# Weight blocks in rows of 2 KB, later stores and another order of reads in a gated pooling and recurrence block

## The chip, the cores and the metric

The kernel runs on one core of a Trainium2 chip. It is one launch. The metric is the device time of that launch in microseconds, the median of several runs.

## What is computed

One layer of a decoder trunk on 2048 tokens of width 1024. The token row is normalised, scaled and shifted by a condition; one wide projection (7168 columns) gives eight parts; a pooling branch and a gated linear recurrence (8 heads of 128) are each projected to the model width, merged by two sigmoid gates and projected once more. Cut to what matters:

```python
h = rms_norm(x, g_pre) * (1.0 + scale) + shift
(pv, pg, hq, hf, hi, hg, mg_pool, mg_hgrn) = jnp.split(h @ w_in, split_idx, axis=-1)

pooled = multiscale_pool(pv)                      # windows 2, 4, 8, 16: mean - token
pooled = jnp.einsum('bsgc,gcd->bsgd', pooled, pool_w).reshape(b, s, POOL_WIDTH) * pool_scale
branch_a = (pooled * jax.nn.silu(pg)) @ w_pool_o

f = lb + (1.0 - lb) * jax.nn.sigmoid(hf)
o = hgrn2(jax.nn.silu(hq), 1.0 - f, hi, jnp.log(jnp.maximum(f, 1e-30)))
o = rms_norm(o, hgrn_norm_g)                      # per head
branch_b = (o * jax.nn.silu(hg)) @ w_hgrn_o

merged = jax.nn.sigmoid(mg_pool) * branch_a + jax.nn.sigmoid(mg_hgrn) * branch_b
y = merged @ w_out
x = x + gate * rms_norm(y, g_post)
```

All inputs and the output are float32.

## The kernel before

**Products.** Each float32 operand is split in two float32r halves (`split`, L174: ScalarE casts the high half, VectorE subtracts it to get the low half), and a product is three matmuls (`three`, L337). Pairs of blocks are multiplied with seven products in place of eight (`quad`, L592, with the weight sums of `quad_items`, L211; and `rows7`, L906, for whole rows). The seven forms are called B11, B21, T1, T2, T3, B22, T4 in `rows7`.

**Stages.** The tokens are worked in two passes of 1024 (`p` 0 and 1), each with two halves `t` of 512. A pass has the value product `V`, then eight heads. A head has three quads: `fq` (forget and query), `m` (the merge gates, stored after a sigmoid by `m_got`, L864) and `gp` (gate and pooling). The recurrence of a head runs as a generator (`hgrn`, L643) that a tick moves on one step; a head has 21 ticks (`htick`, L1370). Behind the heads come the pool projection (`a_job`, L1017), the recurrence's projection (`b_job`, L1027, or `b_fast`, L1075, in the second pass) and the output product `y` (`y_fast`, L1117), in whose steps the first pass also reads and prepares the x of the second.

**Weights.** Weights come as a list of items that are used in order. `take` (L323) hands out the next one and has the items of the four after it loaded and split. In the first pass a weight block is loaded from the input (`raw_load`), split, used, and for the head quads and the pool projection also stored split (512 KB, `keep`) for the second pass, which reads it back (`again`). An item from `whole_item` (L1207) is loaded two items ahead and split when its turn comes.

**Factor steps.** The weight sums of the row products `y7` and `v7` (first pass) and `b7` (second pass) are made by `row_factors` (L256) as a list of small steps: a load of four blocks, sums and differences on VectorE, and stores to DRAM. The list `behind_heads` is worked off inside the heads, on ticks whose count modulo 5 is 1 or 3; what is left runs behind the last head.

**Order.** A planner orders the instructions of each engine; every plain DMA is issued by SP, in one queue. A store (`store`, L108) waits on SP for its data. `gated` (L111) queues a load behind the last store: `after` gives it an edge to that instruction, which holds for instructions of the same engine.

Of the kernel before, what the change touches and what calls it, by code (L numbers as in the profile page):

```python
# [8 lines left out]
F32 = mybir.dt.float32  # L9
# [9 lines left out]
P = 128  # L19
SEQ = 2048  # L20
D = 1024
T = 512
# [48 lines left out]
@with_exitstack  # L71
def tile_block(ctx: ExitStack, tc: tile.TileContext, x, c, w_ada, b_ada, g_pre, g_post, w_in,
               pool_w, pool_scale, lb_logits, hgrn_norm_g, w_pool_o, w_hgrn_o, w_out,
               ident_d, mask_d, icnt_d, w_pv_t, x_t, out):
    nc = tc.nc
    V, A, G, PE, SP = nc.vector, nc.scalar, nc.gpsimd, nc.tensor, nc.sync
    x, out = x[0], out[0]
# [87 lines left out]

    ko = "(k p) n -> p k n"
    items = []
    made = {}  # L170
    scr = {}
# [39 lines left out]
    def quad_items(key, oa, ob, keep_it):  # L211

        def make():
            base = len(ready)
            if (key, 0) in scr:
                return [lambda i=i: again((key, i), f"{base + i}") for i in range(7)]
            r = {}

            def ld(nm, o, half):
                s = w_in[:, o:o + P].rearrange("(i two p) n -> two p i n", p=P, two=2)[half]  # L220
                r[nm] = raw_load(f"{base}{nm}", (s, P))

            def one(i, nm):
                w = item_split(f"{base + i}", r[nm])
                keep((key, i), w, keep_it)
                return w

            def f0():
                if key in made:
                    r["11"], r["12"] = made.pop(key)  # L230
                else:
                    ld("11", oa, 0)
                ld("21", ob, 0)
                ld("22", ob, 1)
                if "12" not in r:
                    ld("12", oa, 1)
                return one(0, "11")

            def f1():
                r["s1"] = wrp.tile([P, T], F32, tag="wr", name=f"wr{base}s1")  # L240
                V.tensor_tensor(r["s1"], r["21"], r["22"], op=ADD)
                return one(1, "s1")

            def f2():
                V.tensor_tensor(r["21"], r["11"], r["21"], op=SUB)
                V.tensor_tensor(r["11"], r["s1"], r["11"], op=SUB)
                return one(2, "11")

            def f3():
                w = one(3, "12")  # L250
                V.tensor_tensor(r["12"], r["12"], r["11"], op=SUB)
                return w
            return [f0, f1, f2, f3, lambda: one(4, "21"), lambda: one(5, "12"), lambda: one(6, "22")]
        items.append((7, make, None))

    def row_factors(key, src, e, whole=(), skip=()):  # L256

        steps = []
        for i in range(4):
            r = {}  # L260

            def ld(i=i, r=r):
                for nm, k, z in (("11", 0, 0), ("21", 0, 1), ("12", 1, 0), ("22", 1, 1)):
                    r[nm] = utile(f"ra{key}{i}{nm}")
                    SP.dma_start(r[nm], src[(2 * i + k) * P:(2 * i + k + 1) * P, z * T:(z + 1) * T])

            def put(f, nm, i=i, r=r):
                if f in whole:
                    scr[key, f, i] = dram(f"scr_{key}_{f}_{i}", [P, T])
                    store((key, f, i), scr[key, f, i], r[nm])  # L270
                    return
                w = [utile(f"rf{key}{f}{i}{z}", F32R) for z in range(2)]
                split(r[nm], w[0], w[1], e)
                scr[key, f, i] = dram(f"scr_{key}_{f}_{i}", [P, 2 * T])
                for z in range(2):
                    store((key, f, i), scr[key, f, i][:, z * T:(z + 1) * T], w[z].bitcast(F32))

            def sums(r=r, i=i):
                r["s1"] = utile(f"rs{key}{i}")
                tt(r["s1"], r["21"], r["22"], op=ADD, e=e)  # L280

            def sub(o, a, b, r=r):
                tt(r[o], r[a], r[b], op=SUB, e=e)

            nop = lambda: None
            todo = [(None, ld), (None, nop),
                    (0, lambda put=put: put(0, "11")),
                    (None, sums),
                    (1, lambda put=put: put(1, "12")),
                    (2, lambda put=put: put(2, "s1")),  # L290
                    (None, lambda sub=sub: sub("21", "11", "21")),
                    (None, lambda sub=sub: sub("11", "s1", "11")),
                    (3, lambda put=put: put(3, "11")),
                    (4, lambda put=put: put(4, "21")),
                    (None, lambda sub=sub: sub("12", "12", "11")),
                    (5, lambda put=put: put(5, "12")),
                    (6, lambda put=put: put(6, "22"))]
            steps += [g for f, g in todo if f not in skip]
        return steps
# [564 lines left out]
    def m_got(p, j, row, t, u, cx):  # L864
        s = utile(f"sgm{p}_{j}_{row}") if t == 0 else u
        A.activation(s, u, AF.Sigmoid)
        store(("Sd", j, row), cx["Sd"][j, row][:, t, :], s)


    def v_job(p, t, grp, q, cx, hook=None):  # L870
# [246 lines left out]
    def y_fast(p, cx, more_steps):  # L1117
# [10 lines left out]
        behind = []  # L1128

        def got(n, t, tk, src):  # L1130
            if (n, t) == (0, 1):
                x_in(0, tk)
            jy = sp.tile([P, T], BF16, tag="jx", name=f"jy{p}_{t}_{n}_{tk}", bufs=1)
            A.activation(jy, src, AF.Square, scale=1.0 / 32, accum_out=rs[t][tk][:, n:n + 1])
            y = src if n == t else utile(f"y{p}_{t}_{n}_{tk}")
            iy = tt(y, src, cx["gg"][n])
            ys[t, tk, n] = y
            if n != 1 - t:
                return
            r = rs[t][tk][:, 0:1]  # L1140
            G.tensor_scalar(r, r, rs[t][tk][:, 1:2], EPS, op0=ADD, op1=ADD)
            tt(r, r, mh[:, 0:1], op=ALU.pow, e=G)

            def scale():
                tok = p * 8 + t * NT + tk
                for n2 in range(2):
                    y, xx = ys.pop((t, tk, n2)), xr[t, tk, n2]
                    V.scalar_tensor_tensor(xx, y, r, xx, op0=MUL, op1=ADD)
                    o = (out[tok * P:(tok + 1) * P, n2 * T:(n2 + 1) * T], xx)
                    if t == 1 or not fin:  # L1150
                        outs.append((state["use"], *o))
                    else:
                        while outs:
                            store("out", *outs.pop(0)[1:])
                        SP.dma_start(*o)
            with after(iy):
                while behind:
                    behind.pop()()
            behind.append(scale)

        def step(nm, i):
            next_parts(p, nm, i, "m", cx["m32"], cx)
            if nm == ("T2" if fin else "T3"):
                for tk in ((0,), (1,), (2, 3))[i]:
                    x_in(1, tk)
            if fin and (nm, i) == ("T1", 0):
                hold_last()
            more_steps(nm, i)
# [60 lines left out]
    for p in range(NPASS):  # L1229
# [11 lines left out]
                else:  # L1241
                    quad_items(("gp", h), (O_PV if h % 2 == 0 else O_PG) + (h // 2) * P, O_G + h * P, p == 0)
        for j in range(KT):
            plain_item(("a", j), w_pool_o[:, j * P:(j + 1) * P].rearrange(ko, p=P), P, p == 0)
        for j in range(KT if p < NPASS - 1 else 0):
            for half in range(2):
                plain_item(("b", j, half),
                           w_hgrn_o[half * T:(half + 1) * T, j * P:(j + 1) * P].rearrange(ko, p=P), P, False)
        if p == NPASS - 1:
            factor_items("b7")  # L1250
        factor_items("y7", p == NPASS - 1)
# [57 lines left out]
    for p in range(NPASS):  # L1309
# [60 lines left out]
        def htick():  # L1370
            tick()
            every[0] += 1
            if every[0] % 5 in (1, 3):
                once(behind_heads)

        for h in range(NH):
            if 0 < h < NH - 1:
# [40 lines left out]
                once(steps)  # L1418
            if p + 1 < NPASS:
                x_stats(8 + h)  # L1420
        while behind_heads:
            once(behind_heads)

        for j in range(KT):
            if j > 0:
# [27 lines left out]
        if p + 1 < NPASS:  # L1453
            nx = cxs[p + 1]
            early = [lambda t=t: r_row(1, t, nx) for t in range(2)]
            tks = [(t, k) for t in range(2) for k in range(KT)]

            def one(i):
                if i < 16:
                    xt_load(1, *tks[i], nx, gated)  # L1460
                if 1 < i < 18:
                    h_scale(*tks[i - 2], nx)
                if 2 < i < 3 + KT:
                    k = i - 3
                    part(1, ("B11", "B21")[k % 2], k // 2, nx["h32"][0, k], nx)

            early += [lambda i=i: one(i) for i in range(18)]

            def y_step(nm, i):
                once(early)  # L1470

            y_fast(p, cx, y_step)
            while early:
                once(early)
        else:
            y_fast(p, cx, lambda nm, i: None)
# [25 lines left out]
```

## Time and profile before

| | before |
|---|---|
| median of 3 runs | 1775.32 us |
| lowest and highest | 1771.82 and 1777.3 us |
| the profiled execution | 1774.9 us |
| its span | 1773.1 us |
| TensorE, VectorE, ScalarE busy | 98%, 69%, 47% of the span |
| mean DMA rate | 245 GB/s |

The span runs from the first to the last instruction of the profiled execution. A busy share is an average over stages, so it tells little of one stage; the table by stretches and the waits tell where an engine stood still. PE is TensorE's matmuls, PEld its weight loads, DVE is VectorE, ACT ScalarE, POOL GpSimd, and SP the engine that issues DMAs (its queue is SPq). Names such as `whl<-wr` are output and input tiles: `wr` and `wri` are raw weights, `whl` split ones, `sm` sigmoids read back from `Sd`, `xr` rows of x for the residual, `h` columns of x, `rav`, `rab` and `rsv`, `rfb` blocks and results of factor steps, `scr_` the DRAM they go to.

### The profile page before, as it was taken

The numbers are of one execution on the slowest core, as the hardware profiler recorded it, in microseconds if no ns is written. First come the engines' busy times: TensorE is split into PE (matmuls) and PEld (weight loads), VectorE is DVE, ScalarE is ACT, GpSimd is POOL, SyncE is SP. The second block draws the span as 40 slices with busy tenths as digits, with TensorE's granted clock in tenths as the row PEclk, the third lists the DMA queues.
The fourth block names the chain that finished last, engine by engine and source line by source line (L and its number), as shares of the span: only waits on it lengthen the run. The fifth ranks groups of instructions, "written<-read, shape, count | busy, mean of one in ns | idle before, by whom it ended". The sixth has DMA issues, their size and how long they took to land.

```text
span 1773.1 us, 31829 instructions
## 1 busy us (share of the span) xinstructions
PE 1729.8 (98%) x11853; PEld 1417.2 (80%) x11853; DVE 1223.7 (69%) x2538; ACT 825.4 (47%) x1927; POOL 92.9 (5%) x152
## 2 busy tenths in 40 slices
PE   6999999999999998999999999999999999999998
PEld 4788888788888886888878888888887888888886
DVE  3668897888887897666678366556656655665676
ACT  4755656566565564411645245344353343423251
POOL 1100000000100010000020000000000000000002
PEclk9999999999999999999999999999999999999999
DMA  9758877887887869963694786766766766586757
GB/s 315 252 175 305 307 265 254 293 288 269 281 294 259 275 218 319 290 206 107 214 338 150 249 266 214 261 228 218 254 224 224 237 193 207 166 294 204 251 182 263
DMA packets 237748, 434.76 MB, mean 245 GB/s; under 512 B 19693, under 2 KB 102298, under 8 KB 237594
## 3 DMA queue, kind: packets, MB, share of 16 engines
q1 hardware_dynamic: 237594, 432.74, 72.1%
q8 instruction: 93, 1.52, 0.4%
q14 instruction: 61, 0.50, 0.1%
HBM read 266.46 MB, written 166.20 MB: 244 GB/s over the span
## 4 chain that ended last, share of the span: by engine, by line
PE 86%; DMA 8%; DVE 3%; ACT 1%; issue 1%; SPq 1%; POOL 0%; DVEq 0%; ACTq 0%; POOLq 0%
PE pam L335 9%; PE pagp L335 9%; PE pafq L335 9%; PE psB L335 5%; PE pem L335 5%; PE pegp L335 5%; PE pefq L335 5%; PE psA L335 4%; PE ray L335 4%; PE psV L335 3%; PE psa L335 3%; PE po L335 3%; PE raB L335 2%; PE raV L335 2%; PE pbm L335 2%; PE pbgp L335 2%
## 5 line engine op out<-in xcount | busy, mean ns | idle before, releaser
L175 DVE TENSOR_TENSOR whl<-wr,whl 128x512 fp32r<-128x512 f32 x176 | 120.5, 689 | 62.1 <-ACT whl L175 51.4
L175 ACT CAST whl<-wr 128x512 fp32r<-128x512 f32 x176 | 109.1, 622 | 104.0 <-PE psB L335 29.0
L335 PE MATMUL pam<-hT,whl 128*128 128x512 f32 x384 | 129.4, 398 | 0.1
L335 PE MATMUL pagp<-hT,whl 128*128 128x512 f32 x384 | 128.2, 395 | 0.1
L335 PE MATMUL pafq<-hT,whl 128*128 128x512 f32 x384 | 126.0, 389 | 0.0
L699 DVE COPY_PREDICATED PT<-mask,psa 128x256 f32<-128x256 uint8 x160 | 86.1, 547 | 47.1 <-PE psa L335 47.1
L335 PE MATMUL psA<-Ph,whl 128*128 128x512 f32 x256 | 84.2, 402 | 9.5 <-DVE sm L465 8.3
L335 PEld LDWEIGHTS pagp<-hT,whl 128*128 128x128 f32 x384 | 72.1, 188 | 16.3 <-issue 0.5
L335 PEld LDWEIGHTS pam<-hT,whl 128*128 128x128 f32 x384 | 72.1, 188 | 16.2 <-ACT c12m L601 0.6
L335 PE MATMUL psV<-whl,hB 128*128 128x512 f32 x256 | 81.1, 399 | 3.3 <-ACT hB L175 3.3
L335 PEld LDWEIGHTS pafq<-hT,whl 128*128 128x128 f32 x384 | 72.1, 188 | 15.0
L465 DVE TENSOR_TENSOR K<-K,TT 128x256 f32<-128x256 f32 x192 | 80.6, 424 | 0.1
L335 PE MATMUL psB<-Gh,whl 128*128 128x512 f32 x256 | 79.6, 391 | 0.0
L335 PE MATMUL pam<-lT,whl 128*128 128x512 f32 x192 | 75.0, 390 | 0.0
L335 PE MATMUL pagp<-lT,whl 128*128 128x512 f32 x192 | 74.9, 390 | 0.0
L335 PE MATMUL pafq<-lT,whl 128*128 128x512 f32 x192 | 74.7, 389 | 0.0
L175 ACT CAST whl<-wri 128x512 fp32r<-128x512 f32 x44 | 27.4, 623 | 93.3 <-PE raB L335 35.9
L335 PEld LDWEIGHTS psa<-X,K 128*32 128x32 f32 x2816 | 49.5, 110 | 25.5 <-issue 22.7
L335 PEld LDWEIGHTS psA<-Ph,whl 128*128 128x128 f32 x256 | 49.2, 192 | 20.9 <-DVE sm L465 8.5
L335 PEld LDWEIGHTS psV<-whl,hB 128*128 128x128 f32 x256 | 48.2, 191 | 16.4 <-ACT hB L175 4.9
L335 PE MATMUL psa<-X,K 128*32 128x48 f32 (+2 forms) x2816 | 59.9, 208 | 0.0
L809 POOL TENSOR_SCALAR ss<-ss 128x4 f32<-128x4 f32 x32 | 11.1, 347 | 906.3 <-ACT junk L808 906.2
(544 smaller groups left out, 4735.8 us busy)
## 6 DMA issues: line engine op xcount, KB each, us to landing
wr<-in_w_in_dram SPq DMA_DIRECT2D x112, 256.0 KB, 4.6
whl<-scr_y SPq DMA_DIRECT2D x36, 512.0 KB, 4.5
sm<-Sd SPq DMA_DIRECT2D x64, 256.0 KB, 5.3
scr_b<-rfb SPq DMA_DIRECT2D x56, 256.0 KB, 2.5
whl<-scr_b SPq DMA_DIRECT2D x28, 512.0 KB, 3.8
scr_y<-rfy SPq DMA_DIRECT2D x40, 256.0 KB, 2.6
x<-in_x_dram SPq DMA_DIRECT2D x32, 256.0 KB, 4.4
wa<-in_w_ada_dram SPq DMA_DIRECT2D x32, 256.0 KB, 6.1
```

The lines of the kernel that those rows point to most:

```text
L175: return A.copy(hi, src32), (e or V).tensor_tensor(lo, src32, hi.bitcast(F32), op=SUB)
L335: return PE.matmul(o, lhsT=l, rhs=r, start=start, stop=stop, skip_group_check=True)
L465: return (e or V).tensor_tensor(o, a, b, op=op)
L699: V.copy_predicated(dst.rearrange("p (c q) a b -> p c q a b", c=NT), m, src.rearrange("p c (a b) -> p c a b", b=b).unsqueeze(2) .broadcast ...
L809: G.tensor_scalar(ss, ss, 1.0 / P, EPS, op0=MUL, op1=ADD)
```

## The change

- The host lays the blocks of `w_in`, `w_pool_o` and `w_hgrn_o` out so that each load of a 128 x 512 block has rows of 2 KB; before, these loads had rows of 512 bytes.
- The pool projection's weights are no longer stored split. The second pass reads the 256 KB raw block again, through `whole_item`, and splits it again.
- The stores of factor steps are put in a list, `due`, and queued at the start of the next factor step. `v7` has 6 steps for each of its four groups in place of 10. In the first pass factor steps run on ticks whose count modulo 9 is 1, 3, 5 or 7.
- The store of a merge gate's sigmoid is issued by ScalarE.
- In the first pass's `y` product, the eight reads of the next pass's x for `t` 0 come in the first two steps, those for `t` 1 in B22 and T4, with their scaling in T4's last two steps; the residual's x for `t` 0 is read in T4's first two steps, where it was read at the end of B22.

```diff
             def ld(nm, o, half):
-                s = w_in[:, o:o + P].rearrange("(i two p) n -> two p i n", p=P, two=2)[half]
-                r[nm] = raw_load(f"{base}{nm}", (s, P))
+                r[nm] = raw_load(f"{base}{nm}", (w_quad[o // P, half], None))
...
+    due = []
+
+    def factor_step(steps):
+        while due:
+            store("due", *due.pop(0))
+        once(steps)
+
     def row_factors(key, src, e, whole=(), skip=()):
...
-                    store((key, f, i), scr[key, f, i], r[nm])
+                    due.append((scr[key, f, i], r[nm]))
...
-                    store((key, f, i), scr[key, f, i][:, z * T:(z + 1) * T], w[z].bitcast(F32))
+                    due.append((scr[key, f, i][:, z * T:(z + 1) * T], w[z].bitcast(F32)))
...
+            if whole:
+                steps += [ld, nop, both(sums, lambda put=put: put(2, "s1")),
+                          lambda sub=sub: sub("21", "11", "21"),
+                          both(lambda sub=sub: sub("11", "s1", "11"), lambda put=put: (put(4, "21"), put(3, "11"))),
+                          both(lambda sub=sub: sub("12", "12", "11"), lambda put=put: put(5, "12"))]
+                continue
...
         A.activation(s, u, AF.Sigmoid)
-        store(("Sd", j, row), cx["Sd"][j, row][:, t, :], s)
+        last["st"] = A.dma_start(cx["Sd"][j, row][:, t, :], s)
...
         def got(n, t, tk, src):
-            if (n, t) == (0, 1):
+            if fin and (n, t) == (0, 1):
                 x_in(0, tk)
...
+            if nm == "T4" and not fin and i < 2:
+                for tk in (2 * i, 2 * i + 1):
+                    x_in(0, tk)
...
         for j in range(KT):
-            plain_item(("a", j), w_pool_o[:, j * P:(j + 1) * P].rearrange(ko, p=P), P, p == 0)
+            if p == 0:
+                plain_item(("a", j), w_po[j], None, False)
+            else:
+                whole_item(lambda j=j: w_po[j])
...
-                plain_item(("b", j, half),
-                           w_hgrn_o[half * T:(half + 1) * T, j * P:(j + 1) * P].rearrange(ko, p=P), P, False)
+                plain_item(("b", j, half), w_ho[j, half], None, False)
...
-            if every[0] % 5 in (1, 3):
-                once(behind_heads)
+            if (every[0] % 9 in (1, 3, 5, 7)) if p == 0 else (every[0] % 5 in (1, 3)):
+                factor_step(behind_heads)
...
-        while behind_heads:
-            once(behind_heads)
+        while behind_heads or due:
+            factor_step(behind_heads)
...
-            tks = [(t, k) for t in range(2) for k in range(KT)]
-
-            def one(i):
-                if i < 16:
-                    xt_load(1, *tks[i], nx, gated)
-                if 1 < i < 18:
-                    h_scale(*tks[i - 2], nx)
-                if 2 < i < 3 + KT:
-                    k = i - 3
-                    part(1, ("B11", "B21")[k % 2], k // 2, nx["h32"][0, k], nx)
-
-            early += [lambda i=i: one(i) for i in range(18)]
+            def x_half(k):
+                part(1, ("B11", "B21")[k % 2], k // 2, nx["h32"][0, k], nx)
+
+            def load4(n):
+                for k in range(4 * n, 4 * n + 4):
+                    xt_load(1, 0, k, nx, gated)
+
+            def one(k):
+                if k < KT:
+                    h_scale(0, k, nx)
+                if k > 0:
+                    x_half(k - 1)
+
+            early[0:2] = [lambda f=f, n=n: (load4(n), f()) for n, f in enumerate(early)]
+            early += [lambda k=k: one(k) for k in range(KT + 1)]
+
+            def load2(n):
+                for k in (2 * n, 2 * n + 1):
+                    xt_load(1, 1, k, nx, gated)
 
             def y_step(nm, i):
                 once(early)
+                if nm == "B22":
+                    load2(i)
+                if nm == "T4":
+                    if i == 0:
+                        load2(3)
+                    else:
+                        for k in range(4 * i - 4, 4 * i):
+                            h_scale(1, k, nx)
...
+    feed["w_quad"] = np.ascontiguousarray(
+        feed["w_in"][0].reshape(4, 2, P, -1, P).transpose(3, 1, 2, 0, 4)).reshape(-1, 2, P, T)
+    feed["w_po"] = np.ascontiguousarray(feed["w_pool_o"][0].reshape(4, P, KT, P).transpose(2, 1, 0, 3)).reshape(KT, P, T)
+    feed["w_ho"] = np.ascontiguousarray(
+        feed["w_hgrn_o"][0].reshape(2, 4, P, KT, P).transpose(3, 0, 2, 1, 4)).reshape(KT, 2, P, T)
```

More of the change, by code (lines that the diff above doesn't have):

```diff
@@ L73, in tile_block @@
                pool_w, pool_scale, lb_logits, hgrn_norm_g, w_pool_o, w_hgrn_o, w_out,
-               ident_d, mask_d, icnt_d, w_pv_t, x_t, out):
+               ident_d, mask_d, icnt_d, w_pv_t, x_t, w_quad, w_po, w_ho, out):
     nc = tc.nc
@@ L164, in tile_block @@
     G.memset(mh, -0.5)
-    ko = "(k p) n -> p k n"
     items = []
@@ L285, in row_factors, with both @@
             nop = lambda: None
+            def both(f, g):
+                return lambda: (f(), g())
+            if whole:
[4 more added lines that the diff above has]
+                continue
             todo = [(None, ld), (None, nop),
```

## The prediction

> **What bounds the kernel now.** I read the page first, then the table of engine time by stretch, the waits of TensorE, and last the queue of SP around each wait.
>
> ```profile
> span 1773.1 us, 31829 instructions
> PE 1729.8 (98%) x11853; PEld 1417.2 (80%) x11853; DVE 1223.7 (69%) x2538; ACT 825.4 (47%) x1927; POOL 92.9 (5%) x152
> ```
>
> TensorE is busy 98% of the span, and the diff touches no matmul. So the change can only win time in which TensorE stands still or runs slowly, and it can lose time by making TensorE wait anew. The next view is that table, first in 25 us stretches, then in 5 us ones. Columns: busy time and instruction count of PE, PEld, DVE, ACT and POOL, then granted TensorE clock, DMA share and GB/s.
>
> ```profile
> 25.00:50.00 25.00, 23.71 (x123) 15.34 (x124) 8.71 (x23) 10.27 (x18) 0.00 (x0) 0.93 1.06 353
> 700.00:725.00 25.00, 16.01 (x76) 12.99 (x71) 11.15 (x18) 5.52 (x12) 0.00 (x0) 0.80 0.99 316
> 750.00:775.00 25.00, 25.00 (x112) 20.72 (x111) 17.40 (x28) 5.49 (x9) 0.21 (x1) 1.00 0.72 234
> 1325.00:1350.00 25.00, 22.32 (x208) 17.29 (x207) 11.60 (x23) 5.43 (x13) 0.00 (x0) 0.93 0.73 260
> 1550.00:1575.00 25.00, 24.26 (x221) 19.15 (x220) 13.87 (x29) 7.49 (x17) 0.00 (x0) 1.00 0.95 326
> ```
>
> ```profile
> 700.00:705.00 5.00, 1.40 (x15) 0.86 (x9) 3.52 (x7) 0.78 (x3) 0.00 (x0) 0.98 0.86 333
> 705.00:710.00 5.00, 0.00 (x0) 0.00 (x0) 0.79 (x2) 0.00 (x0) 0.00 (x0) 0.50 0.88 292
> 710.00:715.00 5.00, 4.61 (x11) 3.64 (x12) 3.53 (x6) 1.24 (x2) 0.00 (x0) 0.50 1.01 334
> 915.00:920.00 5.00, 1.38 (x5) 0.51 (x4) 4.28 (x7) 1.43 (x2) 0.00 (x0) 0.99 1.03 397
> 920.00:925.00 5.00, 4.71 (x15) 3.84 (x16) 2.21 (x4) 1.38 (x4) 1.00 (x3) 0.67 0.92 302
> 1330.00:1335.00 5.00, 2.77 (x12) 1.93 (x11) 3.40 (x10) 0.59 (x1) 0.00 (x0) 1.00 0.98 338
> 1335.00:1340.00 5.00, 4.55 (x13) 3.60 (x14) 0.00 (x0) 0.00 (x0) 0.00 (x0) 0.66 0.53 217
> ```
>
> A stretch at full speed holds 112 wide matmuls in 25 us, or 0.223 us each. There are three holes. Each has idle time and, behind it, matmuls at half clock, which cost their own length once more.
>
> **Hole 1, at 702:** idle 3.60 + 5.00 + 0.39 = 9.0 us; then 11 matmuls in 4.61 us that are worth 11 x 0.223 = 2.45, so 2.2 more. Price 11.2 us. **Hole 2, at 915:** idle 3.62 + 0.29 = 3.9; 15 matmuls in 4.71 us, worth 3.35, so 1.4 more. Price 5.3 us. **Hole 3, at 1333:** idle 2.23 + 0.45 = 2.7; 13 in 4.55 us, worth 2.9, so 1.6 more. Price 4.3 us. The row from 1550 adds 0.7 us of idle time at full clock. The start (the row from 25 us, DMA share 1.06) loads inputs that the change leaves alone.
>
> The waits of TensorE name the four (us in total, times, longest):
>
> ```profile
> PE psA L335 <- DVE sm L465: 8.3, 1, 8.3
> PE ray L335 <- DMA whl<-scr_y: 4.2, 3, 3.6
> PE pbgp L335 <- DMA whl<-scr_('gp', 4)_3_5195: 2.7, 1, 2.7
> PE psA L335 <- DMA whl<-scr_a: 0.7, 1, 0.7
> ```
>
> **Factor steps and stores: hole 1.** A head has 21 ticks, so 8 heads have 168. With the old rule (counts 1 and 3 of 5) 68 of them run a factor step. In the first pass there are 4 x 11 steps for `y7` and 4 x 10 for `v7`, 84 in all; 16 are left and run in one burst behind the heads. SP's queue shows it, and the VectorE row shows who pays.
>
> ```profile
> 696.60 0.95 SPq L265 DMA_DIRECT2D rav<-in_w_in_dram  x2
> 703.29 0.32 SPq L109 DMA_DIRECT2D scr_v<-rsv  x1
> 704.74 1.29 SPq L109 DMA_DIRECT2D scr_v<-rav  x3
> 706.12 1.99 SPq L114 DMA_DIRECT2D sm<-Sd  x4
> ```
>
> ```profile
> 709.65 1.34 DVE L465 TENSOR_TENSOR sm<-psA,sm 128x512 f32<-128x512 f32 x2 [4.21 <-DMA sm<-Sd]
> ```
>
> The last `rav` loads are issued near 697, their stores wait for them until 703 to 705, and the `sm` loads, which the first pool projection needs, stand in the same queue behind those stores until 706. After the change `v7` has 4 x 6 steps, 68 in all, and counts 1, 3, 5, 7 of 9 give 75 slots: the 68th is tick 151, inside the last head. No burst is left, and the `scr_a` stores, which also stood in that queue, are gone. What is late next? The pool weights and `Gl`, on the same queue; nothing shows them without the burst. The gain lies between 11.2 and 11.2 - 4.2 = 7.0 (VectorE would still wait 4.2 for `sm`). I take 10, near the full price, because the row shows the loads landing 3.5 us after issue and the issue is no longer held. The factor work itself does not shrink: 16 steps of `v7` hold some 6 VectorE operations of 0.69 us, 4.4 us that spread over 568 us of heads.
>
> **Stores one step later, sigmoid stores on ScalarE: hole 3.** SP again, with the VectorE row that ends its first wait:
>
> ```profile
> 1312.80 0.52 SPq L114 DMA_DIRECT2D V<-Vd  x1
> 1319.78 0.33 SPq L109 DMA_DIRECT2D scr_b<-rfb  x1
> 1322.16 0.78 SPq L109 DMA_DIRECT2D Sd<-c12m  x1
> 1324.73 3.56 SPq L265 DMA_DIRECT2D rab<-in_w_hgrn_o_dram  x4
> 1328.39 0.39 SPq L197 DMA_DIRECT2D whl<-scr_('gp', 4)_3_5195  x1
> ```
>
> ```profile
> 1319.78 0.69 DVE L175 TENSOR_TENSOR rfb<-rab,rfb 128x512 fp32r<-128x512 f32 x1 [1.43 <-ACT rfb L175]
> ```
>
> ```profile
> 1328.39 7.02 DMA whl<-scr_('gp', 4)_3_5195
> ```
>
> SP is silent for 6.4 us in front of a factor store whose data is made only then; the weight `gp 4_3` is a dozen issues behind and, by the chain of waits, takes until 1335.4. With `due` the store is queued at the next factor step, when its data is old, and three `Sd` stores of this stretch leave SP. SP then arrives 6 us earlier and the missing 2.7 us are covered twice. I take the whole 4.3 (bounds 0 and 4.3: the four `rab` loads stay). The 0.7 us at 1561 is a pool weight of 512 KB loaded from `scr_a` behind such stores; it becomes a prefetched 256 KB load. I take 0.7.
>
> Here the Trainium skill says less. "TensorE: Matmul & The Clock Gate", section "What's actually happening", has the clock halved after an idle window of about 3.4 us; by it hole 3, idle for 2.7 us, would cost no clock, its price would be 2.7 and the sum 1.6 us smaller. The trace differs: a granted clock of 0.66 from 1335 to 1340.
>
> **What ScalarE takes on.** 64 stores, and in the second pass 8 casts with 8 VectorE subtractions for the pool weights.
>
> ```profile
> L109 SPq DMA_DIRECT2D Sd<-sgm x32: 319/320/1579, 159.1 to 1558.5; - x32
> L175 ACT CAST whl<-wr 128x512 fp32r<-128x512 f32 x176 | 109.1, 622 | 104.0 <-PE psB L335 29.0
> ACT c12m L601 <- PE pam L335: 24.8, 10, 3.5
> ```
>
> At SP's 0.32 us an issue that is 20 us over both passes, and 8 x 0.62 = 5 us of casts: ScalarE goes from 47% to 49%. Behind a store stand the PSUM copies of the next product; the third row shows ScalarE idle 24.8 / 10 = 2.5 us ahead of such copies, which hides 0.32 us and also the longest issue, 1.6. No row shows a DMA issued by ScalarE; the bounds are 0 and what is over 2.5 us. I take 0. `gated` orders loads behind `last["st"]`; if that is an instruction of ScalarE, SP's loads are held by nothing: a rival below.
>
> "DMA: Bandwidth & Descriptors", section "Issuing engines are not separate DMA queues", has the Trainium skill speak against this move: another issuing engine saves only issue time, since the transfers share the engines. By that alone hole 3 would stay and the sum be 4.3 smaller. The trace shows a queue held by a semaphore, not by bandwidth.
>
> **Rows of 2 KB.** Of these 112 weight loads 88 have rows of 512 bytes now (24 products of heads with four blocks each, less 8 blocks that are formed on the chip), and so have the 24 of the pool and recurrence projections.
>
> ```profile
> wr<-in_w_in_dram SPq DMA_DIRECT2D x112, 256.0 KB, 4.6
> wri<-in_w_in_dram SPq DMA_DIRECT2D x12, 256.0 KB, 2.7
> 66.00:705.00 639.00, 633.84 (x4899) 522.18 (x4897) 533.31 (x1142) 376.36 (x878) 39.44 (x47) 1.00 0.78 267
> ```
>
> Landing may fall from 4.6 towards 2.7 us, but the loads run four weights ahead and TensorE hides them: from 66 to 705 it idles 5.2 us, of which 3.6 is the beginning of hole 1. At most 1.6 is there; I take 0.
>
> **The reads of x: hole 2.** The weight of T4 is behind eight `xr` loads:
>
> ```profile
> 905.72 6.23 SPq L114 DMA_DIRECT2D xr<-in_x_dram  x8
> 912.94 1.04 SPq L197 DMA_DIRECT2D whl<-scr_y  x2
> 922.00:957.00 35.00, 34.35 (x149) 28.06 (x149) 34.07 (x56) 17.58 (x35) 4.70 (x8) 0.98 0.61 201
> DVE y L465 <- ACT jy L1134: 3.2, 1, 3.2
> ```
>
> The change puts these loads behind T4's weights, and moves eight reads of `x_t` ahead into B11. Hole 2 should go. But VectorE is full behind it, 34.07 of 35 us, and feeds the value product. If TensorE comes 5.3 us sooner, VectorE wins only its own wait of 3.2 (for ScalarE behind the late T4) and gets about four `h_scale` multiplications of 0.69 us more, since all eight of the second half now stand in T4's last steps: 3.2 - 2.8 = 0.4. The bounds are 0.4 and 5.3; I take 2, nearer to the full VectorE row.
>
> **Sum.** 10 + 4.3 + 0.7 + 2 = 17.0. The profiled execution took 1774.9 us (span 1773.1), 0.4 below the median of 1775.3; 1774.9 - 17.0 = 1757.9, and I predict 1758.
>
> **Rivals.** *All holes close*, hole 2 with VectorE keeping up, and the 1.6 us too: 11.2 + 4.3 + 0.7 + 5.3 + 1.6 = 23.1, so 1752. For it: other stretches run at full clock with VectorE as full. Against: the row from 922. *Hole 1 stays in part*: the ungated loads (`sm`, `Pl`, `Gl`) go ahead of weights on SP, VectorE or TensorE waits 7 us at the first pool projection and hole 2 moves to the value product: 4.2 + 4.3 + 0.7 = 9.2, so 1766. For it: DMA share 0.99 from 700 to 725. *The edits do nothing that counts*, as the queue rule above would have it for hole 3, with hole 1 refilled by the loads it delayed: 1775. *Slower: ScalarE held at its issues.* [...] It decides from 2.5 us an issue. At 3.2 us, twice SP's longest, each of 64 stores costs 0.7, 45 in all: 1758 + 45 = 1803; from 3.0 on the kernel is slower than before. Against: SP's median of 0.32.
>
> **Chances and range.** Forecast 0.50, all holes close 0.17, hole 1 stays in part 0.15, nothing 0.09, slower 0.09. Times within 0.3% (1770 to 1781) can't be told from no change. Faster takes the first two and most of the third, 0.80; same 0.11 (the case of nothing and the rest of the third); slower 0.09. The range runs from 1748, a little under all holes closed (the issue time that SP saves may remove smaller waits), to 1773, which takes in 1766 and part of the case of nothing.
>
> **What would show it.** Right: no `sm` wait over 1 us behind the heads, PE over 24.5 in the stretch from 700, no weight wait in the second pass's heads, granted clock 1.00 in both, `scr_v` stores all inside the heads, ScalarE near 49%. VectorE at 34 of 35 us with a TensorE wait for `hT` or `whl` at the value product would show the 2 us right. Wrong: a TensorE wait for a ScalarE copy (`c12m`, `pbgp`) that grew, issues on ScalarE's queue over 1 us, or a new hole at the first pool projection.

## The result and the profile after

The changed kernel takes 1757.07 us (median of 4 runs, 1756.55 to 1757.8); the kernel before took 1775.4 on the same chip. The ratio is 0.9899, with a 95% interval of 0.9882 to 0.9917. The profiled execution took 1757.04 us, 17.9 less than the 1774.9 of before. The forecast was 1758.

The page of the changed kernel, and its table of engine time in 25 us stretches (busy time and count of PE, PEld, DVE, ACT and POOL, granted clock, DMA share, GB/s):

```profile
span 1755.3 us, 31783 instructions
PE 1724.7 (98%) x11853; PEld 1413.7 (81%) x11853; DVE 1229.3 (70%) x2546; ACT 828.6 (47%) x1935; POOL 90.7 (5%) x152
```

```profile
700.00:725.00 25.00, 25.00 (x140) 21.63 (x139) 14.00 (x29) 9.69 (x32) 1.20 (x2) 1.00 0.70 228
900.00:925.00 25.00, 20.58 (x83) 16.10 (x82) 21.82 (x36) 12.07 (x25) 8.29 (x10) 0.93 0.89 313
1325.00:1350.00 25.00, 25.00 (x227) 20.42 (x226) 18.78 (x40) 9.21 (x21) 0.00 (x0) 1.00 0.64 214
1550.00:1575.00 25.00, 25.00 (x180) 21.27 (x179) 18.14 (x36) 6.63 (x16) 0.00 (x0) 1.00 0.59 195
```

Holes 1 and 3 and the 0.7 us at the second pass's pool projection are gone: TensorE is busy throughout the stretches from 700, 1325 and 1550, at full clock. The kernel runs up to 18 us ahead there, so the stretches before count too: those from 1300 and 1525 are also full, and the one from 675 has 0.8 us of idle time, a wait for ScalarE at the first pool projection (`psA <- Ph` below, 0.5 before). The stretch from 900 still holds a hole. TensorE's waits say what it is now:

```profile
PE raV L349 <- DVE y L479: 4.4, 1, 4.4
PE rxV1T L349 <- DVE rcV L479: 1.1, 1, 1.1
PE psA L349 <- ACT Ph L174: 0.8, 1, 0.8
PE raB L349 <- DMA whl<-scr_b: 0.7, 1, 0.7
...
PE pafq L349 <- ACT c12fq L615: 0.3, 1, 0.3
```

The wait for the weight of T4 (`ray <- whl`) is away; in its place the value product `raV` waits for VectorE's `y`, which empties the PSUM banks it needs. The same table in 5 us gives its price, and VectorE's instructions in order of time (start, duration, idle time before in brackets) the reason:

```profile
905.00:910.00 5.00, 1.67 (x8) 1.05 (x6) 2.25 (x4) 4.16 (x11) 3.93 (x8) 1.00 1.04 390
910.00:915.00 5.00, 3.91 (x10) 2.88 (x11) 5.00 (x9) 1.29 (x2) 0.00 (x0) 0.66 1.05 391
```

```profile
901.99 1.29 DVE L479 TENSOR_TENSOR h<-h,rr 128x512 f32<-128x512 f32 x2
...
904.16 0.69 DVE L479 TENSOR_TENSOR h<-h,rr 128x512 f32<-128x512 f32 x1 [0.28 <-DMA h<-in_x_t_dram]
905.56 0.69 DVE L479 TENSOR_TENSOR h<-h,rr 128x512 f32<-128x512 f32 x1 [0.70 <-DMA h<-in_x_t_dram]
908.44 0.69 DVE L174 TENSOR_TENSOR whl<-wri,whl 128x512 fp32r<-128x512 f32 x1 [2.19 <-ACT whl L174]
909.05 1.28 DVE L479 TENSOR_TENSOR h<-h,rr 128x512 f32<-128x512 f32 x2
910.26 0.68 DVE L479 TENSOR_TENSOR y<-ray,gg 128x512 f32<-128x512 f32 x1
```

Idle 3.33 + 1.09 = 4.4 us, and 10 matmuls that are worth 2.2 us took 3.9: 6.1 us, a little more than the 5.3 of hole 2. Six of the eight `h_scale` multiplications stand here ahead of the first `y`, with waits for the reads of x and, through a weight's split, for ScalarE between them.

### The profile page after: what moved, and what is told of

Same layout as the page of the kernel before. It is cut to its first block, busy times and chain, and to the rows that moved or that the text cites. A ratio compares the mean times of both kernels' runs of the same rounds, so it can differ in the third digit from the quotient of the medians.

```text
span 1755.3 us, 31783 instructions
## 1 busy us (share of the span) xinstructions
PE 1724.7 (98%) x11853; PEld 1413.7 (81%) x11853; DVE 1229.3 (70%) x2546; ACT 828.6 (47%) x1935; POOL 90.7 (5%) x152
## 2 busy tenths in 40 slices
DMA packets 193588, 428.47 MB, mean 244 GB/s; under 512 B 19565, under 2 KB 44826, under 8 KB 193434
## 4 chain that ended last, share of the span: by engine, by line
PE 90%; DMA 5%; DVE 3%; ACT 1%; issue 1%; SPq 0%; POOL 0%; DVEq 0%; ACTq 0%; POOLq 0%
PE pagp L349 10%; PE pam L349 10%; PE pafq L349 10%; PE pegp L349 5%; PE psA L349 5%; PE psB L349 5%; PE pefq L349 5%; PE pem L349 5%; PE ray L349 4%; PE psa L349 4%; PE psV L349 3%; PE po L349 3%; PE pbgp L349 2%; PE pbm L349 2%; PE pbfq L349 2%; PE raB L349 2%
## 5 line engine op out<-in xcount | busy, mean ns | idle before, releaser
L174 ACT CAST whl<-wri 128x512 fp32r<-128x512 f32 x52 | 32.1, 622 | 116.4 <-PE raB L349 36.8
L707 DVE COPY_PREDICATED PT<-mask,psa 128x256 f32<-128x256 uint8 (+1 forms) x96 | 52.3, 545 | 7.8 <-PE psa L349 7.8
L349 PEld LDWEIGHTS psA<-Ph,whl 128*128 128x128 f32 x256 | 48.0, 188 | 11.2 <-ACT Ph L174 1.2
```

The lines of the kernel that those rows point to most:

```text
L174: return A.copy(hi, src32), (e or V).tensor_tensor(lo, src32, hi.bitcast(F32), op=SUB)
L349: return PE.matmul(o, lhsT=l, rhs=r, start=start, stop=stop, skip_group_check=True)
L707: V.copy_predicated(dst.rearrange("p (c a) b -> p c a b", c=NT), m.unsqueeze(1).broadcast_to(shp), src.unsqueeze(2).broadcast_to(shp))
```

## The experiments

Each ratio is to runs of the kernel before on the same chip. Waits are TensorE's, in us: total, times, longest.

**e1, one edit alone: the pace and the grouped steps**, with stores queued at once.

```diff
...
-            if every[0] % 5 in (1, 3):
+            if (every[0] % 9 in (1, 3, 5, 7)) if p == 0 else (every[0] % 5 in (1, 3)):
...
```

The grouped steps of `v7` are those of the diff of the change.

> The kernel before with only the factor steps changed: v7 in 6 steps a group, 4 of 9 ticks in the first pass, stores still queued at once. Theory (the burst behind the heads makes hole 1): the wait for sm behind the heads falls from 8.3 us to under 1, hole 3 and hole 2 stay, time 10 us less (ratio 0.994). Rival (hole 1 needs the later stores or the freed queue as well): sm still waits 4 us or more, time 0 to 5 us less.

Measured: 1768.13 us, ratio 0.9968 (0.9956 to 0.998), 5.7 us less. The wait for `sm` is gone from the list; hole 3 stays. Its waits, and three stretches:

```profile
PE pbgp L351 <- DMA whl<-scr_('gp', 4)_3_5217: 2.9, 1, 2.9
PE pagp L351 <- DVE c22gp L481: 2.3, 2, 1.2
```

```profile
375.00:400.00 25.00, 23.78 (x166) 18.95 (x166) 18.56 (x38) 11.47 (x24) 0.49 (x1) 1.00 0.91 310
400.00:425.00 25.00, 23.73 (x220) 18.95 (x219) 21.21 (x43) 13.76 (x29) 1.93 (x2) 1.00 0.83 307
600.00:625.00 25.00, 23.88 (x222) 19.07 (x223) 20.89 (x42) 10.27 (x21) 0.00 (x0) 1.00 0.89 308
```

Hole 1 falls to this edit alone, as the theory has it. It is not worth the expected 10. From the first matmul of the heads to the first of the recurrence's projection the profiled execution takes 619.5 us, where it took 625.6 before. That is 6.1 us less, and the hole cost 11.2, so some 5 us are given back. Of these, 1.22 + 1.27 + 1.12 = 3.6 us are idle time of TensorE in these three stretches of the first pass's heads, which had 24.9 us or more each before.

**e2, one edit alone: the list of late stores.**

```diff
...
-                    store((key, f, i), scr[key, f, i], r[nm])
+                    due.append((scr[key, f, i], r[nm]))
...
```

> The kernel before with only the list of late stores: steps and pace as before. Theory (a store that waits for its data holds SP): hole 3 in the second pass closes, 4.3 us less; hole 1 stays, since the burst is still there; ratio 0.9976. Rival (the four rab loads ahead of the weight make hole 3): no change, ratio 1.000.

Measured: 1775.61 us, ratio 1.0009 (1.0 to 1.0018). Hole 1 and hole 3 stay. Its waits, and SP's longest near hole 3:

```profile
PE psA L342 <- DVE sm L472: 8.0, 1, 8.0
PE pbgp L342 <- DMA whl<-scr_('gp', 4)_3_5193: 3.4, 1, 3.4
```

```profile
SPq L109 <- ACT PV L838: 6.5, 1, 6.5
```

SP still stands 6.5 us at the same store. A store that is queued one step later in the program doesn't free SP here, and the trace shows why:

```profile
1317.85 0.64 ACT L175 CAST rfb<-rab 128x512 fp32r<-128x512 f32 x1
1318.51 0.33 SPq L109 DMA_DIRECT2D scr_b<-rfb  x1
```

The cast that makes the store's data ends at 1318.49, and the store goes out at 1318.51. In the kernel before, the cast ended at 1319.76 and the store went out at 1319.78. So the list did not give the store old data: the planner, it seems, issues it as soon as its data is there. What a store with old data would do to hole 3 is not shown by any run.

**e3, one edit alone: the sigmoid stores on ScalarE.**

```diff
-        store(("Sd", j, row), cx["Sd"][j, row][:, t, :], s)
+        last["st"] = A.dma_start(cx["Sd"][j, row][:, t, :], s)
```

> The kernel before with only the sigmoid stores issued by ScalarE. Theory: an issue takes ScalarE about 0.33 us and its cover hides it, so TensorE waits no more for ScalarE's copies; hole 3 may close on its own, as SP is free of three stores there; 0 to 4.3 us less, ratio 0.9976 to 1.000. Rival (loads that gated no longer holds go ahead of weights): new waits of TensorE for weights, ratio over 1.003.

Measured: 1764.42 us, ratio 0.9948 (0.9935 to 0.9961): 9.4 us less, twice what was expected at most. Hole 3 is closed, and hole 1 is partly so. Its waits behind the heads, and SP's queue near hole 3:

```profile
PE psA L335 <- DVE sm L465: 3.1, 1, 3.1
PE pk L784 <- DVE K L465: 2.5, 1, 2.5
```

```profile
1316.85 0.32 SPq L197 DMA_DIRECT2D whl<-scr_('gp', 4)_3_5195  x1
1318.07 0.98 SPq L109 DMA_DIRECT2D Gd<-sgg  x2
1319.10 2.96 SPq L265 DMA_DIRECT2D rab<-in_w_hgrn_o_dram  x4
```

Without the sigmoid stores the weight `gp 4_3` stands ahead of the four `rab` loads; before, it stood behind them. All 14 traces of this study agree: the seven with hole 3 have the weight behind these loads, the seven without it have it ahead. Counted from the load `V<-Vd`, the weight is issued after 9.4 us in place of 15.6. The 6.2 us of difference are about the issues that no longer stand ahead of it, the three sigmoid stores (1.7) and the `Gd` stores with the `rab` loads (4.6). SP's stand of 6.5 us is cut in two as well, since another weight (`gp 4_1`) is now issued in the middle of it. No run moves the weight alone, so that its place is what closes the hole is read from these rows.

This edit does two things: SP no longer waits for sigmoids, and loads behind `gated` are no longer held behind a sigmoid store. Two kernels part them. **e5, the store on ScalarE, the gate kept at SP's last store:**

```diff
-        store(("Sd", j, row), cx["Sd"][j, row][:, t, :], s)
+        A.dma_start(cx["Sd"][j, row][:, t, :], s)
```

> The kernel before with the sigmoid stores issued by ScalarE, but the last store that gated waits behind stays SP's own. Theory A (what e3 won is SP's waits for sigmoids): as e3, ratio 0.995, hole 3 closed. Theory B (what e3 won is that loads are no longer held behind a sigmoid store): ratio near 1.000, hole 3 as before.

Measured: 1764.96 us, ratio 0.9953 (0.9938 to 0.9968). There is no wait for `gp 4_3`. Behind the heads it is as in the kernel above, with 2.6 us for `K` and this one:

```profile
PE psA L335 <- DVE sm L465: 3.1, 1, 3.1
```

**e6, the store on SP, but nothing held behind it:**

```diff
-        store(("Sd", j, row), cx["Sd"][j, row][:, t, :], s)
+        SP.dma_start(cx["Sd"][j, row][:, t, :], s)
```

> The kernel before with the sigmoid stores still on SP, but gated no longer holds loads behind them. Theory A (waits on SP): ratio near 1.000. Theory B (loads held): ratio 0.995, hole 1 partly and hole 3 closed.

Measured: 1775.23 us, ratio 1.0009 (0.9999 to 1.002), all holes as before:

```profile
PE psA L335 <- DVE sm L465: 7.4, 1, 7.4
PE pbgp L335 <- DMA whl<-scr_('gp', 4)_3_5195: 3.4, 1, 3.4
```

So the gain comes from taking the stores out of SP's queue; what the gate holds is worth nothing that can be measured.

**e7, the changed kernel with the sigmoid stores back on SP.**

```diff
-        last["st"] = A.dma_start(cx["Sd"][j, row][:, t, :], s)
+        store(("Sd", j, row), cx["Sd"][j, row][:, t, :], s)
```

> The changed kernel with the sigmoid stores back on SP. Theory A (SP's waits for sigmoids delay weights): holes in the heads of both passes come back, above all the one at gp 4 of the second pass, 4 to 8 us more, ratio to before 0.993 to 0.995. Rival (the late stores and the pace suffice): 1757, ratio 0.990.

Measured: 1763.5 us, ratio 0.9941 (0.9921 to 0.996). Hole 3 is back although the list of late stores is there, and so are small waits in the first pass's heads like those of the pace alone:

```profile
PE pbgp L349 <- DMA whl<-scr_('gp', 4)_3_5215: 3.2, 1, 3.2
PE pagp L349 <- DVE c22gp L479: 1.8, 2, 0.9
PE pafq L349 <- ACT c12fq L615: 1.0, 1, 1.0
```

**e8, the changed kernel without the late stores.**

```diff
-                    due.append((scr[key, f, i], r[nm]))
+                    store("due", scr[key, f, i], r[nm])
...
```

> The changed kernel with the factor stores queued at once again. Theory (e2: late stores do nothing alone, but they spare the small waits that the faster pace brought in e1 at 398, 406 and 615): up to 5 us more than 1757, ratio to before 0.990 to 0.993. Rival (the sigmoid stores on ScalarE spare them already): 1757, ratio 0.990.

Measured: 1758.87 us, ratio 0.9917 (0.9901 to 0.9932), which overlaps with the 0.9882 to 0.9917 of the changed kernel. There is no new wait in the heads; the one at the value product is 1.0 longer:

```profile
PE raV L349 <- DVE y L479: 5.4, 1, 5.4
```

By the medians, from two chips, the late stores are worth 1.8 us, by the ratios some 3, and by the intervals it may be nothing. The waits that the pace brought are spared without them; they come back in e7 with the sigmoid stores on SP, so it is these stores on ScalarE that spare them, as the rival has it.

**e9, rows of 2 KB and the pool weights read twice**, nothing else.

```diff
-                r[nm] = raw_load(f"{base}{nm}", (s, P))
+                r[nm] = raw_load(f"{base}{nm}", (w_quad[o // P, half], None))
...
+            if p == 0:
+                plain_item(("a", j), w_po[j], None, False)
+            else:
+                whole_item(lambda j=j: w_po[j])
...
```

> The kernel before with rows of 2 KB for all three weights and the pool weights read twice, nothing else. Theory (these loads are covered four weights ahead): hole 1 and hole 3 stay, the 0.7 us wait for scr_a goes; 0 to 1.6 us less, ratio 0.999 to 1.000. Rival (fewer bytes and packets let SP's queue run sooner): hole 1 shrinks with the missing scr_a stores, 3 us or more less, ratio 0.998 or lower.

Measured: 1767.04 us, ratio 0.9952 (0.9937 to 0.9967), 7.7 us less: the rival. Its waits, the stretch behind the heads, and SP's `sm` loads there:

```profile
PE pbgp L334 <- DMA whl<-scr_('gp', 4)_3_5195: 3.1, 1, 3.1
PE pk L783 <- DVE K L464: 1.7, 2, 1.3
PE psA L334 <- DVE sm L464: 1.2, 1, 1.2
```

```profile
700.00:725.00 25.00, 22.93 (x113) 19.17 (x114) 16.37 (x32) 7.67 (x15) 0.00 (x0) 0.93 0.95 342
```

```profile
696.79 2.25 SPq L109 DMA_DIRECT2D scr_v<-rav  x3
699.13 1.86 SPq L114 DMA_DIRECT2D sm<-Sd  x4
```

Hole 1 shrinks from 9.0 us of idle time in that stretch to 2.1. The burst of factor steps is still there, with its stores ahead of the `sm` loads, but the `scr_a` stores are gone from the queue and the last `scr_v` stores go out from 697 in place of 705. Whether the rows or the pool weights do more of it was not tried apart.

**e4, the order of the reads of x alone**, on the kernel before.

```diff
...
+            if nm == "T4" and not fin and i < 2:
+                for tk in (2 * i, 2 * i + 1):
+                    x_in(0, tk)
...
```

> The kernel before with only the reads of x in the first pass's output product moved. Theory (what TensorE wins at T4's weight it pays back behind the eight h_scale in T4's last steps): the wait for scr_y goes, a wait of about 4.4 us for VectorE's y at the value product comes; 0 to 2 us less, ratio 0.999 to 1.000. Rival (the order itself wins hole 2): 5 us less, ratio 0.997.

Measured: 1775.45 us, ratio 1.0011 (1.0001 to 1.0021), so nothing is won. The wait for the weight of T4 is gone and this one has come:

```profile
PE raV L335 <- DVE y L465: 5.7, 1, 5.7
```

**e10, the changed kernel with the old order.**

```diff
-            if fin and (n, t) == (0, 1):
+            if (n, t) == (0, 1):
                 x_in(0, tk)
...
```

> The changed kernel with the reads of x in the order of before. Theory (e4: the new order wins nothing): the wait for the weight of T4 is back, the wait for y at the value product gone, 1756 to 1759, ratio to before 0.989 to 0.991. Rival (with the other holes closed the new order is worth 2 us or more): over 1759.

Measured: 1758.24 us, ratio 0.9904 (0.9889 to 0.9919), not to be told from the changed kernel; the hole is back at the weight of T4:

```profile
PE ray L349 <- DMA whl<-scr_y: 5.1, 3, 4.3
```

**e11 and e12, two versions of the changed kernel in which the eight scalings of `t` 1 don't stand at T4's end.** Their reads move ahead with them. In e11, the reads are in T1 and T2's first step and the scalings in T2's last step and T3; in e12, whose diff is shown, the reads are in T2 and T3's first step and the scalings in B22:

```diff
-                if nm == "B22":
+                if nm == "T2":
                     load2(i)
-                if nm == "T4":
-                    if i == 0:
-                        load2(3)
-                    else:
-                        for k in range(4 * i - 4, 4 * i):
-                            h_scale(1, k, nx)
+                if (nm, i) == ("T3", 0):
+                    load2(3)
+                if nm == "B22":
+                    for k in ((0, 1, 2), (3, 4, 5), (6, 7))[i]:
+                        h_scale(1, k, nx)
```

> The changed kernel with the eight reads of x for t 1 in T1 and the first step of T2, and their scaling in T2's last step and in T3. Theory (the eight scalings stand in front of y on VectorE in T4's end, and that is the wait of 4.4 us): the wait goes and little comes in its place, 4 to 6 us less than the changed kernel, ratio to before 0.987. Rival (the residual's reads in T4 are late, whoever stands in front): the wait stays over 3 us, 1756 to 1758.

> The changed kernel with the eight reads of x for t 1 in T2 and the first step of T3, their scaling in B22. Theory: as in e11, 4 to 6 us less than the changed kernel, unless the reads meet the eight residual reads of T3 and hold a weight, then 1757 or more. Rival (the residual's reads in T4 are late): no gain, as in e11.

Measured: 1754.04 us, ratio 0.9887 (0.987 to 0.9904), and 1753.55 us, ratio 0.9878 (0.9863 to 0.9892). The first has no wait at the value product's start, and a new one at T3 for a scaling on ScalarE; the second keeps a short one and waits for a weight in B22. One row of the first, two of the second:

```profile
PE ray L349 <- ACT h L569: 1.9, 1, 1.9
```

```profile
PE rxy0B L349 <- DMA whl<-scr_y: 1.6, 1, 1.6
PE raV L349 <- DVE y L479: 1.4, 1, 1.4
```

The scalings, with the reads that they wait for, are what held `y` back: the residual's reads are where the change put them, and the wait falls from 4.4 us to 0 and 1.4. The scalings and their own reads were not moved apart. The second version is the fastest kernel of this study, about 21 us under the kernel before and about 3.5 under the changed one, which ran on another chip; by the intervals of the ratios this last figure is not certain. On one chip it can be set against the old order of reads (e10): 1753.06 to 1754.13 us against 1757.53 to 1758.95, so 4.7 us of hole 2 can be won. The profiles agree: from the first matmul of the first pass's `y` product to the first of the second pass's heads, e11 and e12 take 159.7 and 158.9 us, the old order 163.0 to 164.5 in its eight traces, and the changed kernel's order 162.6 to 165.1 in its four.

## Why the prediction was right, point by point

**The sum was right, two of its reasons were not, and part of its closeness is luck.** 17.0 us were forecast and the profiled executions differ by 17.9, their spans by 17.8. The table parts the span at the first matmul of each product:

| Part of the span, us | before | after | won | forecast |
|---|---|---|---|---|
| up to the first pass's heads | 126.1 | 124.5 | 1.6 | 0 |
| first pass's heads and pool projection (hole 1) | 625.6 | 614.7 | 10.9 | 10 |
| recurrence's projection | 88.9 | 88.8 | 0.1 | 0 |
| `y` product and the next value product (hole 2) | 163.0 | 162.6 | 0.4 | 2 |
| second pass's heads (hole 3) | 554.9 | 550.3 | 4.6 | 4.3 |
| second pass's pool projection | 54.1 | 53.0 | 1.1 | 0.7 |
| second pass's recurrence's projection | 76.3 | 77.2 | -0.9 | 0 |
| the rest | 84.2 | 84.2 | 0.0 | 0 |

Hole 2 gave 1.6 us less than forecast, and 1.6 us more came from the part before the heads, where the forecast had nothing. The changed kernel and the five made from it differ in the program only behind this point, and they begin the heads anywhere from 123.4 to 126.6 us, so these 1.6 us lie within the spread of single executions. The 0.9 us lost in the second pass's recurrence's projection, where a wait of 0.7 us for a weight (`raB <- whl`, above) is new, were not forecast either.

**Hole 1, 10 us: right in size and place.** The stretch from 700 is full, no wait for `sm` is left, the last `scr_v` store is issued at 631 us, inside the heads, and the pace alone closes the hole. The step missed that hole 1 has more than one cause: SP's queue was too long there, and each of three edits (the pace, the sigmoid stores, the rows with the pool weights) shortens it, wholly or in part. It also missed the price of the faster pace, some 5 us, which the other edits, the sigmoid stores among them, take away again.

**Hole 3, 4.3 us: right in size, wrong in cause.** The part won 4.6 us, so the hole cost clock beside its 2.7 us of idle time. The step named the late stores first and the three `Sd` stores beside them. It held that with `due` the store's data is old when SP comes to it. It is not: the late stores alone change nothing (SP stands 6.5 us as before, and the store leaves as its cast ends), and with them the hole comes back as soon as the sigmoid stores are on SP again. The edit that closes it is the sigmoid stores. The step took SP's longest wait near the hole for its cause. In the rows the weight was late by its place in the queue, behind the `rab` loads, and the edit that closes the hole moved that place.

**Rows of 2 KB, 0, and the pool weights, 0.7: mis-sized as edits of their own.** Together they are worth 7.7 us on the kernel before. By its profile 7.0 of them lie in the first pass's heads and pool projection, nearly all in hole 1, and 1.1 in the second pass's pool projection, whose 0.7 us wait is gone in e3 as well. The bound of 1.6 was read from the stretch up to 705, and their effect lies mostly behind it. In the changed kernel the pace has closed hole 1 already, so the sum didn't show the error.

**Hole 2, 2 us: the mechanism was right and the size too large.** TensorE's hole moved from the weight of T4 to the value product because the eight scalings stand ahead of `y`. The hole itself went from 5.3 to 6.1 us by its rows, the part of the span that holds it is 0.4 us shorter, and by the runs the two orders can't be told apart. The lower bound, 0.4, was the better value. The sign that was named for the 2 us, a TensorE wait for `hT` or `whl` at the value product, did not come: the wait is for `y`. That VectorE is full behind the hole was not what bound it: with the scalings moved, the same VectorE work leaves a wait of 0 to 1.4 us.

**ScalarE, 0: right.** An issue takes 0.33 us, and the longest wait of TensorE for a PSUM copy of a head is 0.3 us (`pafq <- c12fq`, above). ScalarE is at 47% as before, where 49% was forecast; the forecast counted the issues as busy time, and the page does not:

```profile
L881 ACTq DMA_DIRECT2D Sd<-sgm x32: 326/326/350, 157.0 to 1540.8; - x32
L881 ACTq DMA_DIRECT2D Sd<-c22m x16: 326/327/362, 162.8 to 1536.4; - x16
L881 ACTq DMA_DIRECT2D Sd<-c12m x16: 326/326/356, 167.2 to 1538.9; - x16
```

The rival of a held ScalarE falls with the longest issue of these rows, 0.36 us, the rival of the freed loads with the two kernels on the gate (e5 and e6). The Trainium skill, in "DMA: Bandwidth & Descriptors", section "Issuing engines are not separate DMA queues", would have had this edit save issue time alone. The runs show 9.4 us from 64 stores. Near hole 3 the three stores' own issues are 1.7 us, less than the 2.7 us for which TensorE stood there, and the weight is issued 6.2 us sooner: more than issue time left its way, since the order of SP's queue changed too.

## What to carry to other kernels

In a kernel whose engine is full, look for the queue that feeds its holes, and count what stands in that queue ahead of the late transfer; the longest wait near the hole is not yet its cause. Look in the trace whether an edit has moved what it was meant to move: here a store that was queued later in the program went out at the same moment, as its data came. A store that waits for another engine can cost the issuing queue its order; here it paid to issue it from the engine that makes the data. Work that is moved to free a transfer should not land ahead of the instruction that empties the accumulator.

## What the runs showed of the hardware

**Issues on ScalarE did not lengthen under load.** The 64 issues took 0.33 to 0.36 us each (rows above), while in the same execution an issue on SP took up to 1.1:

```profile
L114 SPq DMA_DIRECT2D sm<-Sd x64: 319/423/1117, 689.1 to 1650.4; - x64
```

**Rows of 2 KB gave no shorter landing that can be told from the spread.** The median from issue to landing is 4.6 us with rows of 2 KB in the changed kernel. The group of before, also 4.6, mixes loads with rows of both sizes, so here are the weight loads of the first pass's heads alone (130 to 640 us). With rows of 512 bytes their median is 5.0 us in the kernel before, 4.6 in e1 and 4.7 in e3; with rows of 2 KB it is 4.5 in e9 and 4.6 in the changed kernel. Packets fell from 237748 to 193588; the stores of the pool weights that are gone have a part in that.

```profile
DMA packets 193588, 428.47 MB, mean 244 GB/s; under 512 B 19565, under 2 KB 44826, under 8 KB 193434
wr<-in_w_quad_dram SPq DMA_DIRECT2D x88, 256.0 KB, 4.6
```
